# Low parts of a third of the output weights formed by an adding transfer

## The chip, the cores and the metric

The kernel runs on one core of a Trainium2 chip. A core has a matrix engine (TensorE, PE in the profile; its weight loads are PEld), an elementwise engine (VectorE, DVE), an activation engine (ScalarE, ACT), a general engine (GpSimd, POOL) and an engine that here only issues transfers (SyncE, SP). Each works through its own instructions in order; semaphores order them against each other. Transfers between HBM and SBUF run on 16 DMA engines. The metric is the device time of one execution in microseconds, as the median of several runs; lower is better.

## What is computed

The reference is a two-layer backbone on 512 latent tokens and 256 context tokens of width 1024. Each layer is half-step SwiGLU, a token mixer, and again half-step SwiGLU, each with modulation before it and a layer norm after it. The part that matters here is the half-step feed-forward, of which the latent tokens go through four:

```python
def swiglu(h, w_in, w_out):
    gate, up = jnp.split(h @ w_in, 2, axis=-1)
    return (jax.nn.silu(gate) * up) @ w_out

def post_norm_update(x, y, m, k, g, b):
    return layer_norm(DN_ALPHA * x + m[..., 3 * k + 2, :] * y, g, b)

def macaron_half_ffn(x, m, k, w_in, w_out, g, b):
    return post_norm_update(x, 0.5 * swiglu(modulate(x, m, k), w_in, w_out), m, k, g, b)
```

The hidden width is 2816, so `w_out` is 2816 x 1024. All values are float32.

## The kernel before, in words

Matmuls run in a reduced float32 form (fp32r). To keep accuracy every operand is split into a high part, its value rounded to that form, and a low part, the value minus the high part. A product then takes three matmuls (`mm3`, lines 146 to 150): high by high on L148, high by low on L149, low by high on L150. In the output phases the first operand is the hidden state (hs) and the second the weights (w), so L149 is the first that reads the low part of w.

`split` makes the two parts: ScalarE writes the high part (L135), then VectorE subtracts it from the source (L136). `unit` (lines 139 to 144) loads one unit of weights, 128 x 1024 values or 512 KB, from SyncE's queue into one of three raw buffers, and splits it into one of six w buffers.

The product with `w_out` is an output phase (class `OutPhase`). Its output has two halves of 512 columns (hf), and each half goes through 11 units (kk), each of two blocks of 128 hidden rows. For one unit, PE runs 4 token blocks x 2 row blocks x 3 matmuls = 24 matmuls of 128 x 512. `operands` makes a unit's weights and splits the two hidden blocks (hs) that belong to it; `part` issues its matmuls; `lead` does this for unit after unit, and after each lets `mod_step` issue some work on modulation: a 512 KB row block of `mod_w` (rawu or mraw) is loaded and multiplied on VectorE (L170). In the three later phases for latent tokens, VectorE also applies the affine part of the layer norm before to x (L350, L351) at the phase's start. At the end of a half, VectorE takes the sums out of PSUM (L357), and behind the second half it normalises, where POOL computes rstd (L371).

Ahead of the three later phases stands an input phase in which the product is made by seven products of block sums (`seven`); ScalarE copies the partial sums out of PSUM (L716), and PE adds on into the same banks behind that copy. The last of these runs while the first output units are being loaded and split, since a scheduler places instructions when the program is built, engine by engine.

The order of the work is thus set by that scheduler and by the buffers: a raw buffer is loaded again when its last reader is done, a w buffer is written again when PE is done with it.

Of the kernel before, what the change touches and what calls it, by code (L numbers as in the profile page):

```python
# [10 lines left out]
F32 = mybir.dt.float32  # L11
F32R = mybir.dt.float32r
BF16 = mybir.dt.bfloat16
I32 = mybir.dt.int32
AF = mybir.ActivationFunctionType
ALU = mybir.AluOpType
AX = mybir.AxisListType

P = 128
# [4 lines left out]
NT = T // P  # L24
# [3 lines left out]
NF = FF // P  # L28
# [42 lines left out]
def backbone_kernel(  # L71
# [27 lines left out]
    nc = tc.nc  # L99

    @contextmanager
    def sbuf(name, bufs, base=0, **kw):
        with tc.tile_pool(name=name, bufs=bufs, reuse_waits="tile", **kw) as pool:
            p = Pool(pool, bufs, base)
            yield p
            p.fill()

    def swap(name, bufs=1):

        return sbuf(name=name, bufs=bufs, side="right")  # L110
# [4 lines left out]
    wpool = ctx.enter_context(sbuf(name="wpool", bufs=1))  # L115
# [18 lines left out]
    def split(dst_hi, dst_lo, src):  # L134
        nc.scalar.activation(dst_hi, src, AF.Copy)  # L135
        latest[0] = nc.vector.tensor_tensor(dst_lo, src, dst_hi.bitcast(F32), ALU.subtract)  # L136
        return latest[0]

    def unit(src, n=1024):
        raw = wpool.tile([P, 1024], F32, tag="raw", name="raw", bufs=3)  # L140
        nc.sync.dma_start(raw[:, :n], src)
        w = wpool.tile([P, 2, 1024], F32R, tag="w", name="w", bufs=6)
        split(w[:, 0, :n], w[:, 1, :n], raw[:, :n])
        return w

    def mm3(ps, a, b, start, stop, **kw):
# [128 lines left out]
    class OutPhase:  # L275
# [13 lines left out]
            self.ys, self.pos = [[], []], [0, 0]  # L289

        def operands(self, hf, kk):
            w = unit(self.units(hf, kk))
            n, hs = self.nt * P, []
            for i in range(2):
                h = self.hget(2 * kk + i)
                if h.dtype != F32R:
                    if self.hsp is None:
                        self.hsp = self.held.enter_context(swap("hsp", self.nhs))
                    s = self.hsp.tile([P, 2, T], F32R, tag="hs", name="hs")
                    split(s[:, 0, :n], s[:, 1, :n], h)  # L300
                    h = s
                hs.append(h)
            return w, hs
# [229 lines left out]
    class FeedIn(Phase):  # L533
# [10 lines left out]
        def load(self, n=None):  # L544
            for _ in range(n or self.nu):
                self.ws.append(unit(self.src(len(self.ws))))
# [28 lines left out]
        def rest(self, hp, nmod):  # L575
            for f in range(len(self.pss) // 2):
                self.evac(hp, self.pss[2 * f], self.pss[2 * f + 1])
            for f in range(len(self.hs), NF):
                pss = []
                for u in range(2):  # L580
                    w = unit(self.src(2 * f + u))
                    ps = bank("psf")
                    feat_mm(ps, w, self.xm, 0, self.n)
                    pss.append(ps)
                self.evac(hp, *pss)
                mod_step(nmod)
                next(self.later, None)
            for _ in self.later:
                pass
            return lambda k: self.hs[k]  # L590

    class Forms:
# [62 lines left out]
        def seven(self, xm, sp, raw0, raw1, sc, early=None):  # L655
# [38 lines left out]
            if early:  # L694
                with tc.issue_after(latest[0].ins):
                    g, u, e = raws()
                    wg = weights(g)
                    next(early)
                    nc.vector.tensor_tensor(e[:, lo], g[:, lo], u[:, lo], ALU.subtract)
                    we = wpool.tile([P, 2, D], F32R, tag="w", name="w", bufs=6)  # L700
                    split(we[:, 0, lo], we[:, 1, lo], e[:, lo])
                    next(early)
                    nc.vector.tensor_tensor(u[:, lo], u[:, hi], u[:, lo], ALU.subtract)
                    nc.vector.scalar_tensor_tensor(e[:, hi], u[:, lo], -1.0, g[:, lo], ALU.mult, ALU.subtract)
                    split(we[:, 0, hi], we[:, 1, hi], e[:, hi])
                    next(early)
                    wu = weights(u)
                    next(early)
                    nc.vector.scalar_tensor_tensor(g[:, lo], g[:, hi], -1.0, e[:, hi], ALU.mult, ALU.subtract)
                    w4 = weights(g, K2)  # L710
            else:
                wg, we, wu, w4 = operands()
# [881 lines left out]
```

## Time and profile before

| | before |
|---|---|
| median of 3 runs | 2452.76 us (2450.28 to 2453.76) |
| the profiled execution's own time | 2451.28 us |
| its span in the profile | 2449.6 us |
| TensorE clock granted | 0.999 |
| DMA, all bytes | 366.01 MB, mean 149 GB/s |
| first matmuls of the four phases | 259.0, 1218.0, 1567.0 and 2321.4 us |

In the profile's rows, `out<-in` names the tiles; `x` with a number is a count; an engine's idle time before an instruction and what ended it stand in brackets in a timeline, and behind the bar in a list of groups. A row of the view of waits reads: who, on which line, waited for whom: us in total, times, longest. Matmul ends are modelled, so PE's pitch is read from the starts of matmuls that follow each other.

### The profile page before, as it was taken

To read this page: it belongs to the slowest core of one execution; us is meant where nothing else is said; L and a number is where in the kernel's file an instruction comes from. 1 tells how busy PE (TensorE), PEld (TensorE's weight loads), DVE (VectorE), ACT (ScalarE), POOL (GpSimd) and SP (SyncE) were. 2 spreads that over 40 slices of the span, in tenths; PEclk is the share of its full clock that TensorE was granted. 3 is DMA by queue.
4 is the path that set the end of the run, shared out by engine and by line. 5 is a ranking of instruction groups with operands and counts; after the bars stand their busy time and mean duration, and the time that the engine had idled before them with its cause. 6 is when DMAs were issued, how large, how long until landed. Compare 5 with 4: busy or idle time off the path is not lost.

```text
span 2449.6 us, 38155 instructions
## 1 busy us (share of the span) xinstructions
PE 2415.6 (99%) x14907; PEld 2185.6 (89%) x14907; DVE 1963.5 (80%) x3532; ACT 1151.4 (47%) x1784; POOL 34.0 (1%) x57
## 2 busy tenths in 40 slices
PE   7999999999999999999999999999999999999998
PEld 5888889987888888999988999988999988999987
DVE  7965679686488886988796988898898777988785
ACT  4222334454454452555643655544654443555641
POOL 0000000000000000000000000000000000000000
PEclk9999999999999999999999999999999999999999
DMA  8866465874211113433474333584323365333452
GB/s 324 299 204 202 164 196 191 285 243 149 70 54 57 61 52 112 152 111 104 139 237 154 108 104 104 156 261 140 122 84 96 116 219 173 132 118 104 138 162 79
DMA packets 107429, 366.01 MB, mean 149 GB/s; under 512 B 12472, under 2 KB 13808, under 8 KB 107248
## 3 DMA queue, kind: packets, MB, share of 16 engines
q1 hardware_dynamic: 107248, 363.58, 45.0%
q8 instruction: 116, 1.90, 0.3%
q14 instruction: 65, 0.53, 0.1%
HBM read 350.92 MB, written 12.61 MB: 148 GB/s over the span
## 4 chain that ended last, share of the span: by engine, by line
PE 83%; DVE 11%; ACT 3%; issue 2%; DMA 1%; POOL 0%; SPq 0%; DVEq 0%; POOLq 0%; ACTq 0%
PE y L150 9%; PE y L148 9%; PE y L149 9%; PE psf L150 6%; PE psf L149 6%; PE psf L148 5%; PE psc L148 5%; PE psc L149 5%; PE psc L150 5%; PE pse L150 3%; PE pse L148 3%; PE pse L149 3%; DVE w L136 1%; PE psa L150 1%; PE psa L149 1%
## 5 line engine op out<-in xcount | busy, mean ns | idle before, releaser
L136 DVE TENSOR_TENSOR w<-raw,w 128x1024 fp32r<-128x1024 f32 (+3 forms) x447 | 502.2, 1128 | 156.4 <-ACT w L135 152.3
L135 ACT ACTIVATE w<-raw 128x1024 fp32r<-128x1024 f32 (+3 forms) x447 | 436.4, 978 | 384.0 <-PE y L150 77.7
L150 PE MATMUL y<-w,hs 128*128 128x512 f32 x984 | 383.5, 390 | 1.2 <-DVE hs L136 1.1
L148 PE MATMUL y<-w,hs 128*128 128x512 f32 x984 | 383.9, 390 | 0.6 <-ACT hs L135 0.6
L149 PE MATMUL y<-w,hs 128*128 128x512 f32 x984 | 382.9, 389 | 0.0
L150 PEld LDWEIGHTS y<-w,hs 128*128 128x128 f32 x984 | 184.6, 188 | 42.0 <-DVE hs L136 3.8
L135 ACT ACTIVATE hs<-h 128x512 fp32r<-128x512 f32 (+1 forms) x220 | 126.4, 587 | 202.4 <-PE y L150 181.7
L148 PEld LDWEIGHTS y<-w,hs 128*128 128x128 f32 x984 | 184.7, 188 | 39.3 <-ACT hs L135 0.9
L149 PEld LDWEIGHTS y<-w,hs 128*128 128x128 f32 x984 | 184.8, 188 | 38.0
L148 PE MATMUL psf<-xm,w 128*128 128x512 f32 (+1 forms) x544 | 191.7, 356 | 14.3 <-ACT xm L1009 10.9
L150 PE MATMUL psf<-xm,w 128*128 128x512 f32 (+1 forms) x544 | 192.1, 354 | 1.2 <-DVE w L136 1.2
L149 PE MATMUL psf<-xm,w 128*128 128x512 f32 (+1 forms) x544 | 192.2, 354 | 0.1
L136 DVE TENSOR_TENSOR hs<-h,hs 128x512 fp32r<-128x512 f32 (+1 forms) x220 | 135.6, 637 | 65.7 <-ACT hs L135 65.5
L148 PE MATMUL psc<-f,w 128*128 128x256 f32 x544 | 154.3, 284 | 0.5 <-ACT sc L716 0.5
L150 PE MATMUL pse<-f,w 128*128 128x256 f32 x544 | 154.2, 284 | 0.1
L148 PE MATMUL pse<-f,w 128*128 128x256 f32 x544 | 154.0, 283 | 0.0
L150 PE MATMUL psc<-f,w 128*128 128x256 f32 x544 | 153.9, 283 | 0.0
L149 PE MATMUL psc<-f,w 128*128 128x256 f32 x544 | 153.9, 283 | 0.0
L149 PE MATMUL pse<-f,w 128*128 128x256 f32 x544 | 153.9, 283 | 0.0
L148 PE MATMUL psc<-xm,w 128*128 128x256 f32 x532 | 151.6, 285 | 0.6 <-ACT sc L716 0.6
L150 PE MATMUL psc<-xm,w 128*128 128x256 f32 x532 | 150.5, 283 | 0.0
L149 PE MATMUL psc<-xm,w 128*128 128x256 f32 x532 | 150.5, 283 | 0.0
(342 smaller groups left out, 6020.1 us busy)
## 6 DMA issues: line engine op xcount, KB each, us to landing
raw<-in_ffn_w_in SPq DMA_DIRECT2D x159, 512.0 KB, 4.6
raw<-in_ffn_w_out SPq DMA_DIRECT2D x110, 512.0 KB, 4.1
mraw<-in_mod_w SPq DMA_DIRECT2D x80, 512.0 KB, 4.6
rawu<-in_mod_w SPq DMA_DIRECT2D x64, 512.0 KB, 3.9
rawu<-in_ffn_w_in SPq DMA_DIRECT2D x60, 512.0 KB, 3.6
x<-x SPq DMA_DIRECT2D x36, 512.0 KB, 4.4
raw<-in_hg_wf SPq DMA_DIRECT2D x32, 512.0 KB, 3.5
raw<-in_cm_w_out SPq DMA_DIRECT2D x24, 512.0 KB, 4.7
```

What stands on the lines that cost most here:

```text
L135: nc.scalar.activation(dst_hi, src, AF.Copy)
L136: latest[0] = nc.vector.tensor_tensor(dst_lo, src, dst_hi.bitcast(F32), ALU.subtract)
L148: nc.tensor.matmul(ps, ah, bh, start=start, stop=False, **kw)
L149: nc.tensor.matmul(ps, ah, bl, start=False, stop=False, **kw)
L150: return nc.tensor.matmul(ps, al, bh, start=False, stop=stop, **kw)
```

## The change

For units 1, 3, 5 and 7 of each half, in the four output phases that have 11 units and four token blocks, `operands` calls `unit_by_sum` in place of `unit`. ScalarE writes the high part as before, and then, in a second pass, the negated high part into the place of the low part. A transfer issued by POOL then reads the same weights from HBM again and adds them onto that tile: weights minus high part. VectorE's subtraction is gone for these units. There are 4 x 2 x 4 = 32 of them, of 88. The raw buffer now has one reader, the high-part pass.

```diff
+    def unit_by_sum(src, n=1024):
+
+        raw = wpool.tile([P, 1024], F32, tag="raw", name="raw", bufs=3)
+        nc.sync.dma_start(raw[:, :n], src)
+        w = wpool.tile([P, 2, 1024], F32R, tag="w", name="w", bufs=6)
+        nc.scalar.activation(w[:, 0, :n], raw[:, :n], AF.Copy)
+        nc.scalar.activation(w[:, 1, :n], w[:, 0, :n].bitcast(F32), AF.Copy, scale=-1.0)
+        nc.gpsimd.dma_start(w[:, 1, :n], src.bitcast(F32R), accum_op=ALU.add)
+        return w
+
...
         def operands(self, hf, kk):
-            w = unit(self.units(hf, kk))
+            w = (unit_by_sum if kk % 2 and kk < 8 and self.nk == NF and self.nt == NT else unit)(self.units(hf, kk))
```

Ten lines are added, so a line from 146 on has a number higher by ten after the change: the high part is L151, the negation L152, the transfer L153.

The scheduler places the new instructions. First, ScalarE where the third of the four phases begins (it starts on PE at 1567 us): before, with w_15541, w_15583, w_15626 and w_15689 the weights of units 0 to 3, sc the copies out of PSUM and silu the input phase's gates.

```order
L769 ACTIVATE silu_15276<-psc_15299 128x256
L135 ACTIVATE w_15583<-raw_15581 128x1024
L716 ACTIVATE sc_15396<-psc_15420 128x256
L716 ACTIVATE sc_15396<-pse_15421 128x256
L716 ACTIVATE sc_15396<-psc_15420 128x256
L135 ACTIVATE w_15626<-raw_15624 128x1024
L135 ACTIVATE w_15689<-raw_15687 128x1024
L716 ACTIVATE sc_15396<-psc_15420 128x256
```

And the same place of ScalarE with the change; w_15599 and w_15706 are now units 1 and 3.

```order
L779 ACTIVATE silu_15292<-psc_15315 128x256
L151 ACTIVATE w_15599<-raw_15597 128x1024
L152 ACTIVATE w_15599<-w_15599 128x1024
L726 ACTIVATE sc_15412<-psc_15436 128x256
L726 ACTIVATE sc_15412<-pse_15437 128x256
L726 ACTIVATE sc_15412<-psc_15436 128x256
L135 ACTIVATE w_15643<-raw_15641 128x1024
L151 ACTIVATE w_15706<-raw_15704 128x1024
L152 ACTIVATE w_15706<-w_15706 128x1024
L726 ACTIVATE sc_15412<-psc_15436 128x256
```

Each negation stands right behind its high part and ahead of a copy out of PSUM. Second, VectorE at the same place, before:

```order
L136 TENSOR_TENSOR w_15541<-raw_15539,w_15541 128x1024
L770 TENSOR_TENSOR h_15277<-h_15277,silu_15276 128x512
L136 TENSOR_TENSOR w_15583<-raw_15581,w_15583 128x1024
L136 TENSOR_TENSOR w_15626<-raw_15624,w_15626 128x1024
L762 TENSOR_TENSOR silu_15397<-psa_15422,sc_15396 128x256
L136 TENSOR_TENSOR w_15689<-raw_15687,w_15689 128x1024
L764 TENSOR_TENSOR h_15398<-sc_15396 128x256
```

And VectorE there with the change:

```order
L136 TENSOR_TENSOR w_15557<-raw_15555,w_15557 128x1024
L780 TENSOR_TENSOR h_15293<-h_15293,silu_15292 128x512
L136 TENSOR_TENSOR w_15643<-raw_15641,w_15643 128x1024
L772 TENSOR_TENSOR silu_15413<-psa_15438,sc_15412 128x256
L774 TENSOR_TENSOR h_15414<-sc_15412 128x256
```

The subtractions of units 1 and 3 are gone, and what stood behind them has moved up; further on the scheduler also puts modulation products and hs subtractions in somewhat other places. Third, POOL's queue around the last two of the four phases, with the change (cve and crs belong to the second layer's mixer):

```order
L153 DMA w<-in_ffn_w_out 128x1024 x8
L381 TENSOR_TENSOR rstd<-ve,neghalf 128x1 x4
L1435 MEMSET tb 128x128
L1427 TENSOR_SCALAR cve_17757<-cmv_17755 128x1
L1429 TENSOR_TENSOR crs_17759<-cve_17757,neghalf 128x1
```

The eight transfers of a phase are together, and behind them come the operations of that phase's end. Before, POOL had no transfers.

## The prediction

> **What bounds the kernel now.** I read the page's first two parts, then PE's waits, then busy time in the half-FFN output phases, then single instructions there.
>
> ```profile
> PE 2415.6 (99%) x14907; PEld 2185.6 (89%) x14907; DVE 1963.5 (80%) x3532; ACT 1151.4 (47%) x1784; POOL 34.0 (1%) x57
> ...
> PE y L150 <- DVE hs L136: 1.1, 2, 0.6
> PE y L148 <- ACT hs L135: 0.6, 1, 0.6
> ```
>
> The first row is the page's; the two below are all that the view of PE's waits has for output-phase matmuls (y): 1.7 us in the whole program. None of them waits for w, the weights. The view of busy time by stretch shows the first 60 us of each phase that the change touches (busy us of PE, PEld, DVE, ACT and POOL with instruction counts, then clock, DMA share, GB/s):
>
> ```profile
> 259.00:319.00 60.00, 60.00 (x267) 49.59 (x266) 41.18 (x77) 23.84 (x32) 0.00 (x0) 1.00 0.53 178
> 1218.00:1278.00 60.00, 60.00 (x267) 49.69 (x266) 59.49 (x119) 28.02 (x39) 0.00 (x0) 1.00 0.74 243
> 1567.00:1627.00 60.00, 60.00 (x266) 49.26 (x265) 59.49 (x124) 27.63 (x39) 0.00 (x0) 1.00 0.76 241
> 2321.00:2381.00 60.00, 60.00 (x269) 49.62 (x268) 53.26 (x96) 27.56 (x40) 0.00 (x0) 1.00 0.55 173
> ```
>
> VectorE is full in two of them (59.49 of 60 us), but PE is full in all. Its busy share alone would not prove that, so the matmuls' pitch must agree. The timeline of PE has
>
> ```profile
> 1567.01 0.40 PE L148 MATMUL y<-w,hs 128*128 128x512 f32 x1
> ...
> 1588.12 0.39 PE L148 MATMUL y<-w,hs 128*128 128x512 f32 x1
> ...
> 1588.80 0.39 PE L148 MATMUL y<-w,hs 128*128 128x512 f32 x1
> 1589.02 0.39 PE L149 MATMUL y<-w,hs 128*128 128x512 f32 x1
> 1589.36 0.50 PE L150 MATMUL y<-w,hs 128*128 128x512 f32 x1
> ```
>
> From 1588.12 to 1588.80 one triple takes 0.68 us, 0.227 us per matmul. 266 of these are 60.3 us, so a 60 us stretch hides no wait of size. A unit is 24 matmuls, 5.44 us. The last row is a wait: due at 1589.25, it started 0.11 us late and took 0.50 us. The weight-load row for this stretch bounds it:
>
> ```profile
> PEld y L150 <- DVE hs L136: 0.6, 2, 0.4
> ```
>
> So TensorE's own pace sets the end, and VectorE's work is taken off an engine on which PE waits 0.6 us at most here.
>
> **The change, part by part.** The groups by form, the DMA issues and one issuing line give the prices:
>
> ```profile
> L136 DVE TENSOR_TENSOR w<-raw,w 128x1024 fp32r<-128x1024 f32 x357 | 436.3, 1224 | 152.3 <-ACT w L135 148.3 <-PE psa L150 3.1
> L135 ACT ACTIVATE w<-raw 128x1024 fp32r<-128x1024 f32 x357 | 376.1, 1054 | 353.4 <-PE y L150 73.6 <-PE psf L150 69.8 <-DMA raw<-in_ffn_w_in 59.4
> ...
> L141 SPq DMA_DIRECT2D raw<-in_ffn_w_out x110: 327/328/334, 218.0 to 2395.3; - x110
> ...
> raw<-in_ffn_w_out SPq DMA_DIRECT2D x110, 512.0 KB, 4.1
> ...
> DMA to landing us min/median/max: 2.7/4.2/9.2
> ```
>
> Removed: one subtraction in units 1, 3, 5 and 7 of each half of four phases, 32 in all, 32 x 1.224 = 39.2 us of VectorE. On the path that sets the end it is worth at most the 0.6 us above, since nothing else there waits for VectorE. The scheduler also puts other VectorE work into the freed places, so I take half: -0.3.
>
> Added on ScalarE: 32 passes of the same form as the high-part pass, 32 x 1.054 = 33.7 us. ScalarE has 60 - 28.0 us free in its fullest stretch, so most are hidden by idle time. The one place where they meet PE is the end of the input phase just before, where ScalarE also empties PSUM for the seven products. Timeline of ScalarE:
>
> ```profile
> 1557.41 1.05 ACT L135 ACTIVATE w<-raw 128x1024 fp32r<-128x1024 f32 x1
> 1558.57 0.38 ACT L716 ACTIVATE sc<-psc 128x256 f32<-128x256 f32 x1
> 1560.01 0.38 ACT L716 ACTIVATE sc<-pse 128x256 f32<-128x256 f32 x1 [1.06 <-PE pse L150]
> ...
> 1561.73 2.22 ACT L135 ACTIVATE w<-raw 128x1024 fp32r<-128x1024 f32 x2
> 1564.33 0.38 ACT L716 ACTIVATE sc<-psc 128x256 f32<-128x256 f32 x1 [0.38 <-PE psc L150]
> ...
> 1565.77 1.15 ACT L135 ACTIVATE hs<-h 128x512 fp32r<-128x512 f32 x2 [0.23 <-PE pse L150]
> ```
>
> Unit 1's new pass goes in ahead of the copy at 1558.57, which then runs from about 1559.6 to 1560.0. PE needs that copy when its product pse ends, at 1560.0 (the next copy waited for it). The margin is about nothing: 0 to 0.3 us late, in each of three phases. If the whole pass of 1.05 us fell on PE it would be 3.2 us. Unit 3's pass comes after the pair at 1561.73 and moves the copy of 1564.33 to about 1565.05, ending at 1565.4; PE needs it when pse ends, about 1565.77: 0.3 us of cover. I take 0.8 us for the three phases, toward the lower bound because the rows leave idle time right behind. The first phase follows plain units without such copies.
>
> Added on the DMA side: 32 transfers of 512 KB that read the weights again, 16.8 MB on 366 MB, from POOL's queue. The wait is new for PE: L149 is the first matmul that reads the low part, and everything on PE is queued behind it. The room in the tightest case, unit 1: its high part ends at 1558.46, the negation at 1559.5; PE starts the phase at 1567.01 and unit 1 at 1572.45, L149 at 1572.7. That leaves 13.2 us. The other two such phases have the same 9.60 us between that pass and their first matmul:
>
> ```profile
> 1208.40 1.05 ACT L135 ACTIVATE w<-raw 128x1024 fp32r<-128x1024 f32 x1
> ...
> 1218.00 0.40 PE L148 MATMUL y<-w,hs 128*128 128x512 f32 x1
> ...
> 2311.77 1.05 ACT L135 ACTIVATE w<-raw 128x1024 fp32r<-128x1024 f32 x1
> ...
> 2321.37 0.40 PE L148 MATMUL y<-w,hs 128*128 128x512 f32 x1
> ```
>
> Later units have more, even where the raw load itself was late:
>
> ```profile
> 1587.98 1.06 ACT L135 ACTIVATE w<-raw 128x1024 fp32r<-128x1024 f32 x1 [3.79 <-DMA raw<-in_ffn_w_out]
> ...
> 1645.98 1.07 ACT L135 ACTIVATE w<-raw 128x1024 fp32r<-128x1024 f32 x1 [2.30 <-DMA raw<-in_ffn_w_out]
> ```
>
> Unit 7 (first row) is due at 1567.01 + 7 x 5.44 = 1605.1, or 15 us after its negation; unit 18, the fourth summed one of the second half (last row), at 1665, or 17 us after. No row shows an adding transfer. From below it is the plain load, 4.1 us; from above three such one after the other (fetch the weights, fetch the tile, write it back), 12.3 us. I take 8.2, since it must read twice the bytes and write once. POOL's issue is between SyncE's 0.33 us and 0.60 us (34.0 us over its 57 instructions). Even 12.3 + 0.6 stays under 13.2. So the wait at L149 costs 0.
>
> [...]
>
> Moved: odd units' raw buffers come free after the high-part pass, not after the subtraction, so SyncE's later loads start earlier. PE does not wait for loads there: 0. POOL's queue has only the rstd operations behind the eight transfers of a phase, and those belong to the phase's end.
>
> Sum: -0.3 + 0.8 + 0 = +0.5 us on the profiled execution's 2451.28, so 2451.8. The median of the runs is 2452.76, 1.48 above that execution; the forecast for a median is **2453.3 us**, no change that can be told. About 0.2% (4.9 us) is what a measurement of this kernel can tell from none.
>
> **Rivals.** *The modulation rows come late (slower).* In the stretch at 1567 the DMA engines are 0.76 busy at 241 GB/s, so 512 KB take 1.65 us of all of them. Five sums start there (units 3, 5, 7, 12, 14): 8.3 us of engine time as plain loads, 16.5 at twice, against 14.4 free. VectorE works in order there and already waits for such loads:
>
> ```profile
> DVE e L170 <- DMA rawu<-in_mod_w: 1.6, 3, 0.6
> ```
>
> Behind a late product stand the hs subtractions, of which PE has just been seen to wait for one. If each of the five holds up one load by 1.65 us, VectorE is 8.3 us later, less the three subtractions saved by unit 7 (3.7): about 4.6 us on PE in this phase, about half of that at 1218 (one load per unit there, not one and a half), nothing in the others: +7, 2460 us. It decides from about 1.4 us of delay per sum, where the loss of both phases, 1.5 x (5 x 1.4 - 3.7), reaches 4.9. Against it: loads are issued earlier, and 24% of the engines' time is free. Chance 0.13.
>
> [...]
>
> *The adding transfer is slower than 12.9 us.* Then L149 of unit 1 waits in three phases. At 20 us, with transfers overlapping, it is 7 us each: 2474 us. Nothing in the rows shows an adding transfer; its plain relative's worst landing is 9.2 us. Chance 0.08.
>
> *The negation lands wholly on PSUM's release.* +3.2 in place of +0.8: 2455.7 us, which still counts as no change. Chance 0.12.
>
> *VectorE's relief is worth more than the waits show (faster).* It would need 4.9 us of waits; the pitch leaves some tenths per stretch and the rows 0.6. Its time would be under 2447.9. Chance 0.06.
>
> **How the numbers follow.** Forecast 0.61, negation on PSUM 0.12, late rows 0.13, slow transfer 0.08, faster 0.06. Same is 0.61 + 0.12 = 0.73; slower 0.13 + 0.08 = 0.21; faster 0.06. The likeliest case alone lies between 2450 (the full 0.6 gained, and the runs' own lowest) and 2456. The range goes on to 2461 to take in the late rows, and leaves out the slow transfer and the faster case, 0.14 together, with a little of the runs' scatter.
>
> **What would show it.** Right: PE's waits name no w L153 and no DMA for y; the waits of y on hs stay under 1 us; VectorE's count falls by 32 and ScalarE's rises by 32; at 1567 VectorE drops from 59.5 to about 55 busy us, or fills up with work that stood later, while PE stays at 60; the DMA share there rises to between 0.85 and 0.95; the landing of the sums is 4 to 12 us. PE waiting for a copy L726 for more than 0.3 us would show the negation's rival; VectorE waiting for rawu with PE behind it on hs, the late rows; L149 waiting for the sum, the slow transfer. A time beyond 2450 to 2456 with none of these rows would make the whole account wrong.

## The result, and the profile after

| | before | after |
|---|---|---|
| median, first comparison (4 runs each) | 2453.26 us (2450.28 to 2454.32) | 2473.43 us (2470.46 to 2475.11) |
| ratio, with its 95% interval | | 1.0083 (1.0065 to 1.0100) |
| the profiled execution's own time and span | 2451.28 and 2449.6 us | 2475.11 and 2473.1 us |
| TensorE clock granted | 0.999 | 0.995 |

The change costs 20 us. The forecast was 2453.3 us and no change; its range ended at 2461. The changed kernel was run again at the end, on another chip:

> The changed kernel once more, beside the kernel before on whatever chip it falls on. If what was found on the first chip holds, it is 18 to 22 us over the kernel before (ratio 1.0075 to 1.009), with VectorE waiting for layer-norm rows (rb) and modulation rows (rawu) and waits of y on hs of about 15 to 20 us in all. If the first comparison was peculiar to its chip, it would come out near 10 us, like the kernels that take away only one of the two suspected causes.

It took 2473.75 us against 2450.65 us there, 23 us and a ratio of 1.0099 (1.0082 to 1.0116), a little above what was expected. PE waits for hs for 16.8 us there. 20 to 23 us is what has to be explained.

The page of the kernel after gives busy times, the two DMA queues, and the shares of the chain that ended last:

```profile
PE 2423.4 (98%) x14907; PEld 2190.3 (89%) x14907; DVE 1928.5 (78%) x3500; ACT 1183.4 (48%) x1816; POOL 62.3 (3%) x89
...
q1 hardware_dynamic: 107248, 363.58, 44.4%
q0 software_dynamic: 4608, 16.78, 3.9%
...
PE 78%; DVE 13%; DMA 4%; ACT 3%; issue 2%; POOL 0%; SPq 0%; DVEq 0%; POOLq 0%; ACTq 0%
```

VectorE has 32 instructions fewer and ScalarE 32 more, so the change does what it says. Of the chain, 4% is now DMA. PE's waits name what PE itself stood for (who, for whom, us in total, times, longest):

```profile
PE y L160 <- DVE hs L136: 17.0, 5, 6.0
...
PE psc L158 <- ACT sc L726: 1.0, 2, 0.6
PE y L158 <- ACT hs L135: 1.0, 2, 0.6
```

L150 of before is L160 now. PE's wait there for the low part of the hidden block (hs, from VectorE) was 1.1 us and is 17.0. No row for y names the weights or their sum (L153): the wait that the change adds never happens. The losses lie inside the three output phases that begin with the affine part of the layer norm. From the starts of each phase's first and last matmul, in the timeline of PE:

| phase | before | after | lost |
|---|---|---|---|
| first | 259.0 to 378.6 | 259.1 to 378.7 | 0 |
| second | 1218.0 to 1338.4 | 1219.1 to 1346.7 | 7.2 |
| third | 1567.0 to 1687.9 | 1575.4 to 1704.7 | 8.4 |
| fourth | 2321.4 to 2441.0 | 2337.6 to 2464.5 | 7.3 |

In sum 22.9 us of the 23.5 by which the two spans differ. In each of the three PE's one long wait (5.3, 6.0 and 4.6 us) stands at unit 4 of the first half. The waits of the stretch from 1217 to 1262 us, of all engines, after:

```profile
PEld y L160 <- DVE hs L136: 5.8, 1, 5.8
PE y L160 <- DVE hs L136: 5.3, 1, 5.3
...
DVE x L361 <- DMA rb<-in_ln_b: 3.7, 1, 3.7
DVE e L180 <- DMA rawu<-in_mod_w: 3.4, 3, 2.2
...
DVE x L360 <- DMA rg<-in_ln_g: 0.6, 1, 0.6
```

Before, the only wait of VectorE for a transfer in that stretch was

```profile
DVE e L170 <- DMA rawu<-in_mod_w: 0.3, 1, 0.3
```

So PE waits for VectorE, and VectorE for rows: the modulation rows (rawu) that the late-rows rival had named, and, more, the scale and shift rows of the layer norm (rg, rb), which it had not. The timelines show the order. First VectorE, after (start, us, line, operation, and in brackets the idle time before it and what ended it):

```profile
1227.27 0.69 DVE L180 SCALAR_TENSOR_TENSOR e<-rawu,e 128x512 bf16<-128x512 f32 x1 [2.23 <-DMA rawu<-in_mod_w]
...
1236.93 1.29 DVE L360 SCALAR_TENSOR_TENSOR x<-x,rg 128x512 f32<-128x512 f32 x2 [0.58 <-DMA rg<-in_ln_g]
1241.89 1.29 DVE L361 SCALAR_TENSOR_TENSOR x<-rb,x 128x512 f32<-128x512 f32 x2 [3.67 <-DMA rb<-in_ln_b]
1243.10 1.29 DVE L360 SCALAR_TENSOR_TENSOR x<-x,rg 128x512 f32<-128x512 f32 x2
1244.31 1.28 DVE L361 SCALAR_TENSOR_TENSOR x<-rb,x 128x512 f32<-128x512 f32 x2
1245.51 0.68 DVE L180 SCALAR_TENSOR_TENSOR e<-rawu,e 128x512 bf16<-128x512 f32 x1
1246.12 0.08 DVE L180 DVE_READ_ACCUMULATOR e<-rawu,e 128x1 f32 x1
1246.12 1.29 DVE L136 TENSOR_TENSOR hs<-h,hs 128x512 fp32r<-128x512 f32 x2
```

The last row makes unit 4's hidden blocks. The three waits above it are 2.23 + 0.58 + 3.67 = 6.5 us. From the start of the phase to that row VectorE runs the same instructions in the same order as before: the subtractions of units 1 and 3 had stood 8.5 and 2.6 us ahead of the phase's start, so nothing of what is saved lies here. The same instruction stood before at

```profile
1238.43 1.29 DVE L136 TENSOR_TENSOR hs<-h,hs 128x512 fp32r<-128x512 f32 x2
```

Before, unit 4's first L150 was due at 1218.0 + 4 x 5.44 + 0.45 = 1240.2 us and its block was ready at about 1239.1: a margin of 1.1 us. Now VectorE is 7.7 us later, PE's phase 1.1 us later, so PE must wait about 7.7 - 1.1 - 1.1 = 5.5 us. POOL's and SyncE's timelines show what the row rb met:

```profile
1226.78 0.86 POOL L153 DMA_DIRECT2D w<-in_ffn_w_out  x1 [8.35 <-ACT w L152]
1233.32 0.88 POOL L153 DMA_DIRECT2D w<-in_ffn_w_out  x1 [5.67 <-ACT w L152]
```

```profile
1232.83 0.33 SPq L282 DMA_DIRECT2D rg<-in_ln_g  x1
1234.03 0.33 SPq L282 DMA_DIRECT2D rb<-in_ln_b  x1
1234.45 2.26 SPq L141 DMA_DIRECT2D raw<-in_ffn_w_out  x2
```

rb is issued 0.7 us behind a sum, and two raw loads follow 0.4 us and about 2 us behind it. The sum landed at 1241.60 us and rb at 1241.80, after 7.8 us, the longest in the view of the tile rb:

```profile
DMA to landing us min/median/max: 4.5/5.9/7.8
```

Before, the same load was issued at 1230.61 us, with no sum ahead of it and the next raw load 2.3 us behind it (SyncE's queue). Its landing is not recorded, but its reader on VectorE started 3.6 us after the issue and had no wait, so it took 3.6 us at most:

```profile
1230.61 0.33 SPq L272 DMA_DIRECT2D rb<-in_ln_b  x1
1232.96 0.33 SPq L141 DMA_DIRECT2D raw<-in_ffn_w_out  x1
```

```profile
1234.20 1.29 DVE L351 SCALAR_TENSOR_TENSOR x<-rb,x 128x512 f32<-128x512 f32 x2
```

Two things have thus moved onto the rows: the sums, and raw loads that are issued earlier, because an odd unit's raw buffer is now free after ScalarE's pass and not after VectorE's subtraction. Busy time by stretch has the same picture (us, busy us of PE, PEld, DVE, ACT, POOL with counts, clock, DMA share, GB/s); the first row is before, the others after:

```profile
1218.00:1240.00 22.00, 22.00 (x99) 18.21 (x98) 21.94 (x44) 11.25 (x18) 0.00 (x0) 1.00 0.53 163
```

```profile
1219.00:1241.00 22.00, 22.00 (x100) 18.23 (x99) 16.41 (x33) 12.79 (x19) 1.75 (x2) 1.00 0.89 235
1241.00:1248.00 7.00, 1.67 (x6) 1.05 (x5) 6.11 (x13) 3.04 (x4) 0.00 (x0) 0.91 0.53 149
1248.00:1250.00 2.00, 2.00 (x6) 1.53 (x5) 2.00 (x7) 0.00 (x0) 0.00 (x0) 0.50 0.93 261
1250.00:1253.00 3.00, 3.00 (x14) 2.46 (x13) 2.51 (x5) 0.00 (x0) 0.00 (x0) 0.98 0.84 253
```

In the 22 us ahead of the wait the DMA engines went from 0.53 to 0.89 busy (from 0.59 to 0.88 and from 0.46 to 0.87 in the first 22 us of the third and fourth phases), and VectorE from 21.94 to 16.41, since it stands and waits. The third row after shows a clock of 0.50 behind the wait, so that the wait costs more than its own length (see the last section). Wait and slow matmuls are 7.1 us: the matmul that was due at 1241.37 started at 1246.86, 5.5 us late, and the eight from there to 1250.31 took 3.45 us in place of 8 x 0.227 = 1.82, 1.6 us.

### The profile page after: what moved, and what is told of

It reads as the page before. It is cut to its first block, busy times and chain, and to the rows that moved or that the text cites. A ratio compares the mean times of both kernels' runs of the same rounds, so it can differ in the third digit from the quotient of the medians.

```text
span 2473.1 us, 38230 instructions
## 1 busy us (share of the span) xinstructions
PE 2423.4 (98%) x14907; PEld 2190.3 (89%) x14907; DVE 1928.5 (78%) x3500; ACT 1183.4 (48%) x1816; POOL 62.3 (3%) x89
## 4 chain that ended last, share of the span: by engine, by line
PE 78%; DVE 13%; DMA 4%; ACT 3%; issue 2%; POOL 0%; SPq 0%; DVEq 0%; POOLq 0%; ACTq 0%
PE y L160 7%; PE y L158 7%; PE y L159 7%; PE psf L160 5%; PE psf L159 5%; PE psf L158 5%; PE psc L158 5%; PE psc L159 5%; PE psc L160 5%; PE pse L160 3%; PE pse L158 2%; PE pse L159 2%; DMA rawu<-in_mod_w 2%; DVE w L136 2%; PE psa L160 1%
## 5 line engine op out<-in xcount | busy, mean ns | idle before, releaser
L136 DVE TENSOR_TENSOR w<-raw,w 128x1024 fp32r<-128x1024 f32 (+3 forms) x415 | 461.8, 1117 | 161.0 <-ACT w L135 160.2
L135 ACT ACTIVATE w<-raw 128x1024 fp32r<-128x1024 f32 (+3 forms) x415 | 402.9, 972 | 379.4 <-PE y L160 90.1
L160 PE MATMUL y<-w,hs 128*128 128x512 f32 x984 | 386.5, 393 | 17.1 <-DVE hs L136 17.0
L159 PE MATMUL y<-w,hs 128*128 128x512 f32 x984 | 385.0, 391 | 0.0
L160 PEld LDWEIGHTS y<-w,hs 128*128 128x128 f32 x984 | 186.4, 189 | 59.2 <-DVE hs L136 20.6
L159 PEld LDWEIGHTS y<-w,hs 128*128 128x128 f32 x984 | 186.1, 189 | 38.7
L160 PE MATMUL psf<-xm,w 128*128 128x512 f32 (+1 forms) x544 | 192.4, 354 | 0.6 <-DVE w L136 0.6
L159 PE MATMUL psf<-xm,w 128*128 128x512 f32 (+1 forms) x544 | 192.7, 355 | 0.1
L160 PE MATMUL pse<-f,w 128*128 128x256 f32 x544 | 154.3, 284 | 0.1
L159 PE MATMUL pse<-f,w 128*128 128x256 f32 x544 | 154.0, 283 | 0.0
L160 PE MATMUL psc<-f,w 128*128 128x256 f32 x544 | 154.0, 283 | 0.0
L159 PE MATMUL psc<-f,w 128*128 128x256 f32 x544 | 153.9, 283 | 0.0
L159 PE MATMUL psc<-xm,w 128*128 128x256 f32 x532 | 150.5, 283 | 0.0
L160 PE MATMUL psc<-xm,w 128*128 128x256 f32 x532 | 150.5, 283 | 0.0
```

The costliest lines, as they stand in the source:

```text
L159: nc.tensor.matmul(ps, ah, bl, start=False, stop=False, **kw)
L160: return nc.tensor.matmul(ps, al, bh, start=False, stop=stop, **kw)
```

## The experiments

Each kernel ran beside the kernel before on its own chip, and ratios are against that. The diffs are against the changed kernel, but for the one that says otherwise.

The theories are these, with the letters that the expectations use. A: the sums' own traffic makes the rows late, those of the layer norm (A1) or those of the modulation (A2). B: every sum costs PE about the same. C: the moved order of instructions or ScalarE's passes do it. D: the earlier raw loads do, which go with any removal of VectorE's reading of raw. Against all: the second reading of the weights is too slow for L159, or ScalarE's negation stands on PSUM's release; of both the trace after shows nothing.

**Fewer sums.** Only in second halves (16), or all but units 5 and 7 of first halves (24).

```diff
-            w = (unit_by_sum if kk % 2 and kk < 8 and ...
+            w = (unit_by_sum if hf and kk % 2 and kk < 8 and ...            # e1
+            w = (unit_by_sum if (hf or kk < 4) and kk % 2 and kk < 8 and ... # e2
```

> Sums only in the second halves (16 of 32). Theory A, the sums of the first halves crowd the rows (modulation, layer norm) for which VectorE waits at the start of three phases, and hs and PE follow: about the time before, 2450 to 2456 us, and PE's wait of y on hs back under 2 us from 17.0. Theory B, every sum costs PE about the same (20 us over 32): about 2463. The 16 subtractions that are gone bring nothing under either, since PE does not wait for them: not under 2449.

> Sums as changed, but units 5 and 7 of the first halves subtract on VectorE again (24 sums stay). Theory A: the transfers in flight when the layer-norm row rb is fetched are those two, so its wait of 2.3 to 3.7 us goes, while the late modulation row behind unit 3's sum (2.2 us) stays: 2453 to 2460 us. Theory B, an equal price per sum: 2468. If units 1 and 3 were what matters: 2470 or more.

Measured: 2454.46 us, 1.0012 (1.0002 to 1.0021), and 2459.35 us, 1.0030 (1.0019 to 1.0041). Both lie in the range of theory A, though e1's wait for hs, 3.2 us, is over the 2 us expected. With none in first halves the second and fourth phases lose nothing and the third 4.2 us, in its second half. With two per first half the three phases lose 1.0, 4.6 and 1.2 us, and the waits of L361 for rb are all but gone (0.3 us) while those for rawu stay. So the sums of the first halves cost most of it, and more than in proportion: 16 sums in second halves cost 2.9 us, 8 more another 4.9, and the last 8 another 12 to 15.

**The sum's size and kind.** The same order of instructions on every engine, but the transfer adds 32 of 1024 columns (e3), or is a plain load of the whole tile that adds nothing (e4).

```diff
-        nc.gpsimd.dma_start(w[:, 1, :n], src.bitcast(F32R), accum_op=ALU.add)
+        nc.gpsimd.dma_start(w[:, 1, :32], src[:, :32].bitcast(F32R), accum_op=ALU.add)   # e3
+        nc.gpsimd.dma_start(w[:, 1, :n], src.bitcast(F32R))                              # e4
```

> All 32 sums, but each adds 32 of the 1024 columns (the rest of the low part stays the negated high part, so the output is not the reference's). The order of instructions on every engine, the negations and the early release of the raw buffers are those of the change. Theory A: 2450 to 2457 us, VectorE's waits for rb and rawu as before the change. Theory C, the moved order on VectorE, the passes on ScalarE or raw loads that start early are the cause: 2470 or more.

> All 32 transfers from POOL's queue, of the same bytes, but plain loads over the negated high part instead of additions (output not the reference's); order as in the change. In the change a sum takes 3.9% of 2473 us over 32, 3.0 us of all 16 engines; a plain load 1.6 us. Theory A with engine time as the price: half the crowding or less, 2455 to 2464 us. If the bytes read from HBM, or the second queue as such, are the price: 2470 or more.

Measured: 2457.44 us, 1.0022 (1.0013 to 1.0032), and 2460.84 us, 1.0035 (1.0020 to 1.0049). The first is just above the range of theory A, the second inside it. POOL's queue in e3 and e4 (packets, MB, share of 16 engines' span; the change's, with 3.9%, stands above):

```profile
q0 software_dynamic: 4608, 0.53, 0.4%
```

```profile
q0 software_dynamic: 4608, 16.78, 2.1%
```

Over 32 transfers, 2.1% of e4's span are 1.6 us of all engines each, 3.9% of 2473.1 are 3.0 us. With next to no traffic from the sums the change still costs 5.9 us, with the plain load 9.2, with the full sum 20 to 23. So traffic is most of it: over e3, the plain load adds 3.4 us and the sum 14 to 17, so that twice the engine time costs about four times as much. What remains without traffic is still a wait for rb; in the stretch from 1217 to 1262 us of e3:

```profile
DVE x L361 <- DMA rb<-in_ln_b: 1.9, 1, 1.9
```

**Raw buffers held.** To tell the earlier raw loads from the order, VectorE reads one column of each odd unit's raw tile, near the place where its subtraction stood, so that the buffer is free only when VectorE has been there; with the narrow sum (e6) and with the full one (e9).

```diff
         nc.scalar.activation(w[:, 1, :n], w[:, 0, :n].bitcast(F32), AF.Copy, scale=-1.0)
+        seen = wpool.tile([P, 1], F32, tag="seen", name="seen", bufs=2)
+        nc.vector.tensor_copy(seen, raw[:, :1])
-        nc.gpsimd.dma_start(w[:, 1, :n], src.bitcast(F32R), accum_op=ALU.add)
+        nc.gpsimd.dma_start(w[:, 1, :32], src[:, :32].bitcast(F32R), accum_op=ALU.add)   # e6 alone
```

> The narrow sums of before (32 of 1024 columns, output not the reference's) with the raw buffer held until VectorE has read one column of it, so the next raw load waits for VectorE again, as before the change. With narrow sums alone 5.9 us of the loss stayed. Theory D, those are raw loads that now start early and meet the layer-norm row: 2450 to 2454 us and the wait for rb under 0.5 us in each phase, from 1.7 to 1.9. Theory C, the order on VectorE or the passes on ScalarE: 2456 to 2460.

> The change with all 32 full sums, and the raw buffer held until VectorE has read one column of it. With narrow sums this took the loss from 5.9 to 1.7 us. Theory D+A, the early raw loads and the sums' engine time add up: 4 to 8 us less than the change, 2465 to 2470 us. If the sums' own crowding is all: 2471 to 2475. If the early raw loads are needed for any harm: 2455 or less.

Measured: 2452.65 us, 1.0005 (0.9995 to 1.0014), and 2464.58 us, 1.0052 (1.0037 to 1.0067). The second is just under the range that was expected for A and D together. With narrow sums the loss is gone, and no row of the stretch from 1217 to 1262 us names rb or rg; what VectorE waits for there is

```profile
DVE e L182 <- DMA rawu<-in_mod_w: 2.8, 2, 2.5
```

So the remainder of e3 was the earlier raw loads, not the order, which up to unit 4's block of this phase is that of the kernel before. With full sums rb is spared too, but rawu is not: 5.1 us of waits in that stretch, and 8.5 us of PE on hs in the whole program. The three phases lose 0.6, 8.4 and 3.8 us: holding raw helps the second and the fourth, and not the third. The four kernels make a table of us over the kernel before of their own chip:

| | raw free early | raw held |
|---|---|---|
| narrow sum | 5.9 (e3) | 1.7 (e6) |
| full sum | 20 to 23 (the change) | 12.8 (e9) |

The early raw loads cost 4 us without the sums' traffic and 7 to 10 with it; the traffic costs 11 us with raw held and 14 to 17 without. That each makes the other worse is suggested only: the intervals of the four ratios are too wide to show it. (1.7 us is not told apart from none.)

**The layer-norm rows.** The second set of rg and rb isn't fetched, and the first is used in its place (e5).

```diff
+            g, b = (load_row(self.bp, tag, src[self.affine][:HC]) for tag, src in (("rg", ln_g), ("rb", ln_b)))
             for hf in range(2):
                 c = slice(hf * HC, (hf + 1) * HC)
-                g, b = (load_row(self.bp, tag, src[self.affine][c]) for tag, src in (("rg", ln_g), ("rb", ln_b)))
```

> All 32 sums, but the layer-norm rows rg and rb are fetched for the first half of the columns alone and used for both (output not the reference's). In the change VectorE waits 10.7 us for the second set in the three phases and 7.9 us for modulation rows. Theory A1, the layer-norm rows carry most of the loss: 2456 to 2462 us. Theory A2, the modulation rows alone would hold VectorE as long: 2466 or more.

Measured: 2463.64 us, 1.0048 (1.0031 to 1.0065), 12.7 us over before: between the two cases of the expectation. In the profiled execution, the fastest of the four (7.9 us over before), the three phases lose 2.2, 4.5 and 2.6 us in place of 7.2, 8.4 and 7.3. What is left is rawu, for instance from 1620 to 1695 us:

```profile
DVE e L180 <- DMA rawu<-in_mod_w: 10.4, 5, 3.5
```

By the medians the second set carries a third to a half of the loss; the rest goes with the modulation rows, the only ones for which VectorE's waits are still longer there than before. Neither alone is the cause. (For the second set the change's rows give 9.1 us on rb and 2.8 on rg, 11.9 in all and not 10.7.)

**The affine part elsewhere.** The computation is whole again: the second set of rows comes five units later, so that rb does not meet units 3 and 5; with the change (e7) and, the same edit on the kernel before, without it (b7).

```diff
                 self.lead(0, 3, nmod)
-                self.finish()
+                self.finish((0,))
+                self.lead(0, 7, nmod)
+                self.finish((1,))
...
-        def finish(self):
+        def finish(self, halves):
-            for hf in range(2):
+            for hf in halves:
```

> All 32 sums in full; the second half of the layer norm's affine part is issued after unit 6 in place of unit 2, so nothing of unit 4's hs stands behind the late row. Theory A1: most of the loss goes, 2452 to 2459 us, PE's wait of y on hs under 5 us from 17.0. Theory A2, modulation rows or the bandwidth are enough: 2463 or more.

> The kernel before with the same later place of the second affine half and no sums. PE waits for hs 0.6 us in those phases before, so at most that is to be had: 2449 to 2453 us. It is the partner of the run with all sums and the later place.

Measured: 2460.81 us, 1.0038 (1.0025 to 1.0051), above what was expected, with 8.7 us of PE on hs and not under 5; and 2451.71 us, 1.0002 (0.9993 to 1.0012), so the place itself is worth nothing to the kernel before. With the change, the second and fourth phases lose nothing at all now, although modulation rows still come late. From 1217 to 1262 us VectorE waits as long as the 6.5 us counted above, and no wait of PE follows:

```profile
DVE e L180 <- DMA rawu<-in_mod_w: 6.5, 2, 4.5
```

Half of the affine part has moved out from ahead of unit 4's block, which is now ready 18.3 us into the phase, with 3.9 us to its first reader. So a late row cost PE only what exceeded the margin behind it: nothing in this phase of e7, 5.3 us in that of the change, where VectorE was 7.7 us later. The whole loss, 8.7 us, is in the third phase, the one with the most rawu loads per unit, by the prediction's count one and a half. Waits of e7 from 1620 to 1695 us:

```profile
DVE e L180 <- DMA rawu<-in_mod_w: 10.5, 3, 4.1
...
PE y L160 <- DVE hs L136: 4.9, 1, 4.9
```

The third phase lost as much in the change, 8.4 us, but at unit 4 of its first half. From 1620 to 1700 us VectorE waited 11.4 us for rawu there and PE not at all for hs, which fits: PE had already been put back at unit 4. Taking away the first wait let the next one through.

**Sums taken out where that loss is.** e7 with the second half of the third phase on VectorE again, 28 sums.

```diff
-... and self.nt == NT else unit)
+... and self.nt == NT and not (hf and (self.l, self.j) == (1, 0)) else unit)
```

> As the run with the later affine half, but the second half of the phase at 1567 us subtracts on VectorE as before (28 sums stay). That run lost 8.5 us there, with VectorE waiting 10.5 us for modulation rows and PE 4.9 us for hs, and nothing in the phases at 1217 and 2330. Theory A: 2450 to 2455 us. If the loss is spread otherwise (a price per sum, or the clock): 2458 or more.

Measured: 2455.54 us, 1.0016 (1.0006 to 1.0025), just above the expected range; the third phase now loses 0.5 us, the others nothing, in the profiled execution (2452.76 us, the fastest of ten). Four sums in one half of one phase were worth 6 us (9.9 less 3.8), and 28 sums cost little once the late rows have a margin behind them. They bring nothing either. The 3.8 us by which the median is still over the kernel before are more than this one profile shows.

**Both remedies.** Raw held, and the affine part later, with full sums.

> All 32 full sums, raw buffer held, affine half later. Theory D+A: what is left are modulation rows in the second half of the phase at 1567 us, with one competitor less: 2453 to 2459 us, below the 2460.8 of the later affine half alone.

Measured: 2463.88 us, 1.0047 (1.0031 to 1.0064): a miss. The two did not add up; it is worse than e7. The second and fourth phases lose nothing, the third 12.2 us, from 1620 to 1695 us:

```profile
DVE e L182 <- DMA rawu<-in_mod_w: 10.6, 4, 8.0
...
PE y L162 <- DVE hs L136: 8.8, 1, 8.8
```

One rawu load took 11.0 us from issue to landing there, against 8.5 us for the slowest in e7. It was issued 2.4 us behind a sum and 1.7 us behind a raw load; the same load in e7 was 3.3 and 3.6 us behind them. That names the row but does not show why holding raw made it later than e7's; this stays open, as does what a second buffer for rg and rb would do. No kernel here beats the kernel before, and by its profile little could: PE waits there for 1.7 us in all its output phases.

## Why the prediction was wrong

*The mechanism was a rival's.* Late rows, with VectorE in order, hs behind them and PE behind hs, had a chance of 0.13 and a price of +7 us. It is what happened, at three times that price, while the forecast's sum had no term for it. The sentence under "Moved" failed first: raw buffers free earlier, SyncE's loads start earlier, "PE does not wait for loads there: 0". PE indeed waits for no load. But an earlier load was here also an earlier rival of loads in flight, and VectorE waits for some of these. Measured: 4 us alone (e3 less e6), 7 to 10 beside full sums. Worse, the earlier issue stood in the text as evidence against the late rows.

*The rows named were too few.* The rival counted rawu loads only. The affine part on L350 and L351 stood in the text on the kernel; its rows rg and rb are read by VectorE in the same order of work, and the second set carries a third to a half of the loss (e5).

*The price of one meeting.* Each sum was to hold one load by 1.65 us, the engine time of a plain 512 KB. A sum takes 3.0 us of all engines, and one rb took 7.8 us where it had taken 3.6 at most. The "24% free" did not protect the rows: the 22 us that decide were emptier than the mean before (0.53 busy in the second phase, 0.59 in the third), and rows were still late in all three phases: VectorE waited 3.7, 3.1 and 2.3 us for rb. And the waits come in strings: 6.5 us of them ahead of one hs.

*The margin was not worked out.* The forecast took PE's small waits (0.6 us) as a sign that VectorE's work has room. A small wait says how late hs was, not how early. Unit 4's block had 1.1 us; VectorE came to it 7.7 us later, and PE waited 5.3 us for it. VectorE's three saved subtractions by unit 7 (3.7 us) were credited against it, though none of them falls between the phase's start and unit 4's block.

*"Nothing in the others."* The rival put most of its loss into the third phase, half as much into the second and none into the fourth, which had a DMA share of 0.55 before. The three lost 8.4, 7.2 and 7.3 us. The affine rows are in all three. The first phase has none and lost nothing, though its first 60 us went from 0.53 to 0.78 busy.

*The clock.* No term had what follows a long wait of PE: 1.6, 2.1 and 2.5 us more at half clock in the three phases.

What held. *L149 has 13.2 us of room:* no PE wait names the sum. The landings are, in the view of line 153,

```profile
L153 POOL DMA_DIRECT2D w<-in_ffn_w_out x32: 856/872/1032, 240.0 to 2419.0; - x32
...
DMA to landing us min/median/max: 5.8/7.4/9.4
```

with a median of 7.4 us near the 8.2 that the author had estimated from plain loads of 4.1, and none over 9.4. POOL's issue is 0.87 us, over the bound of 0.60 that came from its mean instruction, without consequence. So the slow-transfer rival is out. *The negation costs 0.8 us at PSUM:* the wait of psc on its copy is 1.0 us after; before, it was

```profile
PE psc L148 <- ACT sc L716: 1.1, 2, 0.6
```

so the term was 0. The passes themselves took 33.9 us for 32, as costed. *VectorE's relief is worth 0.3 us:* e6, which has nearly all of the relief and next to none of the traffic, gains nothing (1.0005). Of the signs promised for the forecast, three failed with it: hs keeps PE waiting for 17.0 us and not under 1, the share of DMA in the third phase, which now begins at 1575.4, is 0.81 and not 0.85 to 0.95, and VectorE is busy there for 49.95 us and not 55, with PE at 54.01 and not 60:

```profile
1575.40:1635.40 60.00, 54.01 (x231) 44.19 (x229) 49.95 (x107) 29.20 (x40) 2.62 (x3) 0.94 0.81 234
```

The one for late rows, VectorE waiting for rawu with PE behind it on hs, came true.

## What to carry to other kernels

A full engine that is not the bound still holds a margin for the one that is (here 1.1 us): work it out, instruction by instruction, as the time from a result's end to its first reader, before adding anything that could delay that engine, and list every transfer it waits for in order. An earlier free buffer was not free of cost here (4 us alone, 7 to 10 beside full sums): it brought its load forward onto what was in flight, so each moved issue needs a look at what lands beside it. When a transfer takes over arithmetic, price its engine time (here 3.0 us against 1.6 of a load) against each load that is in flight beside it, not against the free share of a phase, and test it at full and at next to no size with the order kept.

## What the runs showed of the hardware

*A sum costs the DMA engines twice a load.* 3.0 us of all engines for 512 KB against 1.6 us for the plain load from the same queue (e4), a ratio of 1.9. No run here shows which part of the transfer it is.

*An adding transfer also takes POOL longer to issue*, 0.87 us against 0.53 for the plain one (medians of 32; in e4):

```profile
L153 POOL DMA_DIRECT2D w<-in_ffn_w_out x32: 527/527/725, 240.1 to 2404.9; - x32
```

The narrow sum took as long as the full one, so it is the adding and not the size (e3):

```profile
L153 POOL DMA_DIRECT2D w<-in_ffn_w_out x32: 856/872/1034, 240.0 to 2401.9; - x32
```

*After a wait of 5.33 us PE runs at half its pace for 3.45 us.* The timeline of PE, after:

```profile
1241.14 0.39 PE L159 MATMUL y<-w,hs 128*128 128x512 f32 x1
1246.86 0.80 PE L160 MATMUL y<-w,hs 128*128 128x512 f32 x1 [5.33 <-DVE hs L136]
...
1248.31 0.63 PE L160 MATMUL y<-w,hs 128*128 128x512 f32 x1
1248.73 0.63 PE L158 MATMUL y<-w,hs 128*128 128x512 f32 x1
...
1250.02 0.46 PE L158 MATMUL y<-w,hs 128*128 128x512 f32 x1
1250.31 0.39 PE L159 MATMUL y<-w,hs 128*128 128x512 f32 x1
```

The pitch is 0.43 us from 1247.45 to 1250.02 and 0.23 afterwards, and the granted clock is 0.50 from 1246.73 to 1250.14, for 3.41 us. In the third and fourth phases, behind waits of 5.99 and 4.55 us, it is 0.50 for 6.8 us from 1601.71 and from 2362.89, of which 4.4 and 5.2 us fall on matmuls. The price of these stretches is 1.6, 2.1 and 2.5 us: 6 of the 23 us lost. Shorter waits were followed by it too: behind one of 3.01 us of PE for x (L401, at 987.50 us, after) the granted clock is 0.50 from 987.3 to 990.7, and behind one of 1.93 us (e9, fourth phase, which lost 3.8 us) from 2357.02 to 2360.44. Behind one of 2.33 us (e5, fourth phase) it stays at 1.00; no matmul of y on hs in e5 takes over 0.504 us, while the row of 1248.31 above takes 0.63. So a wait of PE cost up to 2.5 us on top in the change, and its length alone does not tell whether it will.
